# A recurrence inside a projection stream: a full-width state product, and output products issued once per quarter

## The chip, the core and the metric

The kernel runs on one core of one Trainium2 chip. The metric is the device time of one execution in microseconds, from launch to end; lower is better. [...] DMA queues move data between DRAM and SBUF.

## The reference

One layer of a decoder trunk is applied to a prompt of 1024 tokens and to 8 single-token samples, with a model width of 2048. After a norm, one projection (2048 to 8320 columns) feeds two groups of heads. Group A is an RWKV-7 time mixing with 16 heads of 64; group B is a retention with 4 heads of 256. The outputs are mixed, projected back, gated and normed. What the change touches is the recurrence of group A:

```python
def step(S, inp):
    r_t, w_t, k_t, v_t, a_t, b_t = inp
    sa = jnp.einsum('bhvk,bhk->bhv', S, a_t)
    S = S * w_t[:, :, None, :] + sa[..., None] * b_t[:, :, None, :] + v_t[..., None] * k_t[:, :, None, :]
    y = jnp.einsum('bhvk,bhk->bhv', S, r_t)
    return S, y
```

## The kernel before

All big projections are computed as three fp16 products (high times high, high times low, low times high) and run as one stream, the main stream: for each block of 128 output columns there are 3 token groups of 344, and for each of these 16 x 3 matmuls into a bank `pj` (`proj_gen`, `mm3`; the tiles are `u`, `mix` or `hh` for the activations and `whi`, `wlo` for the weights). Everything else is woven into this stream.

The weaving is done when the kernel is built. A `Driver` keeps an estimated clock for every engine. The main stream yields after every three matmuls. Then `poll` runs each background generator that is due: its next instructions are appended to the engines' queues at that place. A generator is due again 0.2 us after the estimated end of what it issued last, on any engine:

```python
b[0] = max(b[2].last + 0.2 if b[2].last else 0.0, self.t + w if isinstance(w, float) else 0.0, self.t)
```

The estimate of a product depends on the columns of its moving operand alone:

```python
n = rhs.free_size()
dv.op("PE", max((4 * n if lhsT.dtype == F32 else n) / 2400.0 + 0.0025, 0.025), [out], [lhsT, rhs])
```

On the chip each engine works through its queue in the written order and waits for semaphores.

Group A is handled in eight pairs of heads, p = 0 to 7. The tokens of a pair form 16 chunks of 64, and four chunks make a quarter. `front_gen` makes the quarters' inputs: `ar` (128 rows: two heads of 64; the first 64 of its 128 columns belong to the decayed removal keys, the last 64 to the receptances), `bk`/`bn` (the keys) and `x` (masked scores, whose triangular part is replaced by an inverse that VectorE solves, with a round trip through DRAM). `uv` holds per chunk the solved vectors u in rows 0 to 63 and the values v in rows 64 to 127.

`chain_gen` is the recurrence, in order over the 16 chunks of a pair. One chunk has three stages with a `yield` between them, so matmuls of the main stream stand between the stages:

1. The state's product (`ch<-Sbd,AR`, 128 rows and 64 columns of weights) is accumulated onto the product of scores and values that was issued one chunk earlier (`a2v`, `ch<-UV,X`). VectorE copies the sum to `R`.
2. The inverse is applied to `R` (`ch<-R,X`), VectorE copies the result into `uv`, and `a2v` of the next chunk is issued.
3. The update product (`ch<-UV,BN`), two VectorE instructions that make the new state `Sbd`, and the products for the output y: state by receptances (`y<-AR,Sbd`) and, for each head, `uv` by scores (`y<-X,UV`). Eight chunks share one bank `y`, which ScalarE and VectorE empty after the eighth.

All these products are fp32. An fp32 product appears in the trace as two matmuls, each with its own weight load. PSUM banks for the chain (`ch`) come from a pool of two, the bank `y` from a pool of one. The rings of `ar`, `x`, `bn` and `uv` come free when a quarter is marked done (`chq`), after its fourth chunk.

Of the kernel before, what the change touches and what calls it, by code (L numbers as in the profile page):

```python
# [10 lines left out]
F32 = mybir.dt.float32  # L11
F32R = mybir.dt.float32r
I32 = mybir.dt.int32
AF = mybir.ActivationFunctionType
ALU = mybir.AluOpType
PSUM = bass.MemoryType.PSUM

P = 128
# [244 lines left out]
def hybrid(ctx, tc, A):  # L263
    nc = tc.nc
    dv = Driver()
    V, S_, G = Eng(dv, "DVE", nc.vector), Eng(dv, "ACT", nc.scalar), Eng(dv, "POOL", nc.gpsimd)
# [3 lines left out]
    def pool(name, bufs=1, space=None, c=None, side=None):  # L270
        kw = {} if space is None else {"space": space}
        if side:
            kw["side"] = side
        return PoolProxy(dv, (c or ctx).enter_context(tc.tile_pool(name=name, bufs=bufs, **kw)), bufs)
# [11 lines left out]
    def mm(out, lhsT, rhs, **kw):  # L286
        n = rhs.free_size()
        dv.op("PE", max((4 * n if lhsT.dtype == F32 else n) / 2400.0 + 0.0025, 0.025), [out], [lhsT, rhs])
        PE.matmul(out, lhsT, rhs, **kw)  # L289
# [515 lines left out]
    two = pool("a2", 2, c=cr, side="right")  # L805
# [41 lines left out]
    def scr(i, dt=F32):  # L847
        return scp.tile([P, HB], dt, name=f"S{i}" if dt == F32 else f"R{i}", tag=f"S{i}")

# [103 lines left out]
    def front_gen(p):  # L953
# [116 lines left out]
        while p and ("chq", 4 * p - 1) not in done:  # L1070
            yield 0.3
        yield from chain_gen(p)

    def bkn_gen(p):
# [59 lines left out]
    def chain_gen(p):  # L1134
        DC = H["dc", p]

        def a2v(c):
            g, ci = 4 * p + c // 4, c % 4
            while ("uv", g) not in done or ("bkn", g) not in done:
                yield 0.3  # L1140
            ps = chp.tile([P, 512], F32, name="ch")
            x, uv = H["x", g], H["uv", g]
            for h in range(2):
                mm(ps[0:64, h * 64:h * 64 + 64], x[64:128, h, ci, 0:64], uv[64:128, ci, h * 64:h * 64 + 64],
                   start=h == 0, stop=c == 0 and h == 1, skip_group_check=True)
            return ps
        nxt = yield from a2v(0)
        for c in range(16):
            hf, g, ci = c // 8, 4 * p + c // 4, c % 4
            x, uv, bn, ar = (H[n, g] for n in ("x", "uv", "bn", "ar"))  # L1150
            if c % 8 == 0:
                ts = slice(hf * HB, hf * HB + HB)
                yps = yp.tile([P, 512], F32, name="y")
            S0, S1 = Sbd[c % 2], Sbd[1 - c % 2]
            ps = nxt
            if c:
                mm(ps[0:64, 0:P], ar[:, ci, 0:64], S0, start=False, stop=True, skip_group_check=True)
            R = two.tile([64, P], F32, name="R")
            V.tensor_copy(out=R, in_=ps[0:64, 0:P])
            yield  # L1160
            for h in range(2):
                mm(ps[0:64, P + h * 64:P + h * 64 + 64], x[0:64, h, ci, 0:64], R[:, h * 64:h * 64 + 64],
                   start=True, stop=True)
            V.tensor_copy(out=uv[0:64, ci, :], in_=ps[0:64, P:2 * P])
            if c < 15:
                nxt = yield from a2v(c + 1)
            yield
            mm(ps[:, 2 * P:3 * P], bn[:, ci, :], uv[:, ci, :], start=True, stop=True)
            for h in range(2):
                hs = slice(h * 64, h * 64 + 64)  # L1170
                src = ps[hs, 2 * P + h * 64:2 * P + h * 64 + 64]
                if c:
                    V.scalar_tensor_tensor(out=S1[hs, hs], in0=S0[hs, hs], scalar=DC[hs, c:c + 1],
                                           in1=src, op0=ALU.mult, op1=ALU.add)
                else:
                    V.tensor_copy(out=S1[hs, hs], in_=src)
            ysl = yps[:, (c % 8) * 64:(c % 8) * 64 + 64]
            if c:
                mm(ysl, S0, ar[:, ci, 64:128], start=True, stop=False, skip_group_check=True)
            for h in range(2):  # L1180
                hs = slice(h * 64, h * 64 + 64)
                mm(ysl[hs], uv[:, ci, hs], x[:, h, ci, 64:128], start=c == 0, stop=True, skip_group_check=True)
            if ci == 3:
                done.add(("chq", g))
            if c % 8 == 7:
                while not (p == 0 and hf == 0) and ("norm", p if hf else p - 1, 1 - hf) not in done:
                    yield 0.3
                Yh = og.tile([P, HB], F32R, name="Yh")
                Yl = og.tile([P, HB], F32R, name="Yl")
                S_.activation(Yh, yps, AF.Copy)  # L1190
                V.tensor_tensor(out=Yl, in0=yps, in1=Yh, op=ALU.subtract)
                done.add(("chain", p, hf))
                dv.spawn(norm(p, hf, Yh, Yl, ts))
            yield
        for h in range(2):
            hs = slice(h * 64, h * 64 + 64)
            SP.dma_start(out=A["o_wkvp"][2 * p + h], in_=Sbd[0][hs, hs])

    def norm(p, hf, Yh, Yl, ts):
        while ("gA", p) not in done:  # L1200
            yield 0.3
        yield when(Yl, 0.1)
        yield "g"
        yc = gtile()
        mm_exact(yc, cent_r, Yh, Yl)
        y2 = og.tile([P, HB], F32, name="y2")
        Y = og.tile([P, HB], F32, name="Y")
        S_.activation(y2, yc, AF.Square)
        S_.activation(Y, yc, AF.Copy)
        Yh = og.tile([P, HB], F32R, name="Yh")  # L1210
        Yl = og.tile([P, HB], F32R, name="Yl")
        halves(y2, Yh, Yl)
        yield when(Yl, 1.4)
        yield "g"
        yv = gtile()
        mm_exact(yv, bones_r, Yh, Yl)
        gt = og.tile([P, HB], F32, name="gt", tag="Yh")
        SP.dma_start(out=gt, in_=d_gate[p][:, ts])
        S_.activation(y2, yv, AF.Ln, scale=1.0 / 64, bias=eps_a[:, 0:1])
        S_.activation(y2, y2, AF.Exp, scale=-0.5)  # L1220
        yield
        V.tensor_tensor(out=Y, in0=Y, in1=y2, op=ALU.mult)
        bo = og.tile([P, HB], F32, name="bo", tag="Yl")
        SP.dma_start(out=bo, in_=d_bon[p][:, ts])
        V.tensor_scalar(out=Y, in0=Y, scalar1=vcol("gn_a_g", p), scalar2=vcol("gn_a_b", p), op0=ALU.mult, op1=ALU.add)
        yield
        G.tensor_tensor(out=Y, in0=Y, in1=bo, op=ALU.add)
        G.tensor_tensor(out=Y, in0=Y, in1=gt, op=ALU.mult)
        SP.dma_start(out=d_mxa[p][:, ts], in_=Y)
        done.add(("norm", p, hf))  # L1230
# [930 lines left out]
```

## Time and profile before

| | |
|---|---|
| median of 3 runs | 2767.7 us (2762.01 to 2771.42) |
| profiled execution | 2758.49 us, span of its instructions 2756.7 us |
| mean granted TensorE clock | 0.981 of full speed |
| TensorE / VectorE / ScalarE / GpSimd busy | 96% / 60% / 40% / 18% of the span |
| the pairs' chains | first `ch<-UV,X` at 269.2 us, last at 1425.6 us |

Busy time is the union of an engine's instructions. Matmuls are pipelined: the next one starts before the printed end of the one before, so what a matmul costs in a full queue is the distance between starts. In the timeline, neighbours of one form are merged into one row with a count; its first number is the start of the first of them, its second the time to the end of the last.

### The profile page before, as it was taken

Reading aid. Unit: us, or ns where it says so; the run is one execution under the profiler, and the core shown is the slowest. Engines: PE = TensorE matmul, PEld = TensorE weight load, DVE = VectorE, ACT = ScalarE, POOL = GpSimd, SP = SyncE. Lnnn points to the kernel's source line nnn. Section 1 sums busy time; section 2 is a strip of 40 time slices with the busy share of each in tenths; the row PEclk is TensorE's granted clock in tenths of the full one; section 3 lists DMA queues with packets and bytes.
Section 4 is the critical chain, followed back from the end, with each engine's and each line's share of the span. In section 5 each row is a group of like instructions: output and inputs, shape, how many; then the busy total and the mean of one; then the engine's idle time right before and its main releaser. Section 6 shows DMA issues by size and latency. Waiting matters only on the chain. (4 is left out here: it accounts for less than half of the span.)

```text
span 2756.7 us, 46895 instructions
## 1 busy us (share of the span) xinstructions
PE 2634.9 (96%) x19480; PEld 1774.0 (64%) x19480; DVE 1662.9 (60%) x3522; ACT 1114.5 (40%) x1563; POOL 508.0 (18%) x558
## 2 busy tenths in 40 slices
PE   7999999999999999999899999999999999999997
PEld 4566666666666666666567667676766666666664
DVE  7568687868577686867544867636365434353334
ACT  7543444343353434434224235443343323344333
POOL 3322122112121222212110321101000000033333
PEclk9999999999999999999899999999999999999998
DMA  7222121312222131222323435616163222333214
GB/s 267 75 79 61 53 82 40 95 35 78 60 85 55 53 99 30 82 60 82 93 78 119 168 134 191 218 66 209 47 223 129 94 106 100 131 123 108 101 69 139
DMA packets 146741, 283.63 MB, mean 103 GB/s; under 512 B 62568, under 2 KB 100520, under 8 KB 131424
## 3 DMA queue, kind: packets, MB, share of 16 engines
q1 hardware_dynamic: 132160, 178.91, 19.7%
q10 hardware_dynamic: 14368, 101.73, 10.9%
q8 instruction: 152, 2.49, 0.4%
q14 instruction: 61, 0.50, 0.1%
HBM read 212.78 MB, written 67.55 MB: 102 GB/s over the span
## 5 line engine op out<-in xcount | busy, mean ns | idle before, releaser
L289 PE MATMUL pj<-u,whi 128*128 128x344 f16 x6176 | 1388.5, 313 | 29.0 <-DVE sgt L244 16.1
L289 PEld LDWEIGHTS <-whi 128*128 128x128 f16 x9408 | 883.1, 99 | 494.7 <-issue 73.0
L289 PE MATMUL pj<-u,wlo 128*128 128x344 f16 x3088 | 959.1, 312 | 0.0
L289 PEld LDWEIGHTS <-wlo 128*128 128x128 f16 x4704 | 463.7, 99 | 233.3 <-DVE wlo L244 1.5
L244 DVE SCALAR_TENSOR_TENSOR wlo<-raw,so,whi 128x512 f16<-128x512 f32 (+1 forms) x398 | 294.1, 772 | 80.8 <-ACT whi L244 80.4
L289 PE MATMUL pj<-hh,whi 128*128 128x344 f16 (+3 forms) x1536 | 335.2, 309 | 0.2 <-ACT whi L244 0.2
L289 PE MATMUL pj<-mix,whi 128*128 128x344 f16 x1504 | 330.8, 310 | 1.5 <-DVE hr L244 1.5
L244 ACT ACTIVATE whi<-raw,so 128x1024 f16<-128x1024 f32 (+2 forms) x200 | 217.6, 1121 | 125.4 <-DVE so L244 118.1
L289 PE MATMUL pj<-hh,wlo 128*128 128x344 f16 (+3 forms) x768 | 237.3, 309 | 0.4 <-DVE wlo L244 0.4
L289 PE MATMUL pj<-mix,wlo 128*128 128x344 f16 x752 | 230.1, 310 | 0.4 <-DVE wlo L244 0.4
L244 ACT ACTIVATE wjunk<-raw 128x2048 f16<-128x2048 f32 x94 | 177.2, 1885 | 100.2 <-DVE raw L244 63.4
L244 ACT ACT_TABLE_LOAD x136 | 174.5, 1283 | 16.5 <-DVE R L244 11.4
L244 POOL TENSOR_TENSOR H<-H,sgt 128x344 f32<-128x344 f32 (+3 forms) x45 | 59.5, 1322 | 552.8 <-DMA xr<-d_ple 363.2
L244 DVE TENSOR_TENSOR tm<-LT,Z 128x8 f32<-128x8 f32 (+15 forms) x128 | 138.7, 1084 | 2.0
L244 ACT ACTIVATE z<-pj,winv 128x344 f32<-128x344 f32 x74 | 40.3, 547 | 240.0 <-PE pj L289 191.1
L244 DVE TENSOR_TENSOR sgt<-sgt,xr 128x344 f32<-128x344 f32 (+3 forms) x48 | 25.8, 538 | 159.5 <-ACT sgt L244 157.6
L244 POOL TENSOR_TENSOR d<-z 128x344 f32<-128x344 f32 (+1 forms) x75 | 63.1, 842 | 253.7 <-ACT z L244 174.4
L244 ACT ACTIVATE sgt<-pj,winv 128x344 f32<-128x344 f32 (+4 forms) x93 | 50.7, 545 | 144.7 <-PE pj L289 128.7
L244 DVE SCALAR_TENSOR_TENSOR Sbd<-Sbd,DC,ch 64x64 f32<-64x64 f32 x240 | 66.4, 277 | 53.5 <-PE ch L289 50.3
L244 DVE SCALAR_TENSOR_TENSOR hr<-pj,winv,xr 128x344 f32<-128x344 f32 x47 | 26.9, 575 | 111.2 <-PE pj L289 107.8
L244 POOL TENSOR_TENSOR rl<-y,rh 128x344 fp32r<-128x344 f32 x24 | 27.2, 1133 | 345.8 <-DVE rh L244 177.0
L244 DVE TENSOR_REDUCE Z<-tm 128x4 f32<-128x8 f32 (+15 forms) x128 | 86.5, 676 | 4.4
(319 smaller groups left out, 3325.4 us busy)
## 6 DMA issues: line engine op xcount, KB each, us to landing
raw<-in_w_in ACTq DMA_DIRECT2D x63, 1024.0 KB, 5.1
raw<-in_w_out ACTq DMA_DIRECT2D x16, 1024.0 KB, 4.8
raw<-in_w_gate ACTq DMA_DIRECT2D x16, 1024.0 KB, 4.8
x<-in_xT SPq DMA_DIRECT2D x16, 516.0 KB, 10.3
tb<-in_rq SPq DMA_DIRECT2D x24, 344.0 KB, 5.0
tb<-in_rk SPq DMA_DIRECT2D x24, 344.0 KB, 3.7
xr<-in_xT SPq DMA_DIRECT2D x16, 516.0 KB, 4.2
d_h<-hr SPq DMA_DIRECT2D x16, 516.0 KB, 2.9
```

The costliest lines, as they stand in the source:

```text
L244: return f(*a, **k)
L289: PE.matmul(out, lhsT, rhs, **kw)
```

## The change

Three edits in `chain_gen`:

- `a2v` closes its accumulation. Except for chunk 0, ScalarE copies its result from PSUM to a new SBUF tile `AV` (64x128).
- The state's product takes all 128 columns of `ar` as weights and writes 128 rows into its own columns of the bank (the last 64 rows aren't read). VectorE makes `R` by adding `AV` to the first 64 rows, in place of a copy.
- The two `y<-X,UV` products of each chunk are no longer issued in that chunk. After the fourth chunk of a quarter, all eight of the quarter are issued. The bank `y` is opened by the first product of state by receptances (chunk 1 or 8) alone, and everything after it accumulates or, on columns not written since, overwrites.

```diff
--- before.py
+++ after.py
@@ -1142,8 +1142,12 @@
             x, uv = H["x", g], H["uv", g]
             for h in range(2):
                 mm(ps[0:64, h * 64:h * 64 + 64], x[64:128, h, ci, 0:64], uv[64:128, ci, h * 64:h * 64 + 64],
-                   start=h == 0, stop=c == 0 and h == 1, skip_group_check=True)
-            return ps
+                   start=True, stop=True, skip_group_check=True)
+            av = None
+            if c:
+                av = two.tile([64, P], F32, name="AV")
+                S_.activation(av, ps[0:64, 0:P], AF.Copy)
+            return ps, av
         nxt = yield from a2v(0)
         for c in range(16):
             hf, g, ci = c // 8, 4 * p + c // 4, c % 4
@@ -1152,11 +1156,13 @@
                 ts = slice(hf * HB, hf * HB + HB)
                 yps = yp.tile([P, 512], F32, name="y")
             S0, S1 = Sbd[c % 2], Sbd[1 - c % 2]
-            ps = nxt
+            ps, av = nxt
+            R = two.tile([64, P], F32, name="R")
             if c:
-                mm(ps[0:64, 0:P], ar[:, ci, 0:64], S0, start=False, stop=True, skip_group_check=True)
-            R = two.tile([64, P], F32, name="R")
-            V.tensor_copy(out=R, in_=ps[0:64, 0:P])
+                mm(ps[:, 3 * P:4 * P], ar[:, ci, :], S0, start=True, stop=True, skip_group_check=True)
+                V.tensor_tensor(out=R, in0=ps[0:64, 3 * P:4 * P], in1=av, op=ALU.add)
+            else:
+                V.tensor_copy(out=R, in_=ps[0:64, 0:P])
             yield
             for h in range(2):
                 mm(ps[0:64, P + h * 64:P + h * 64 + 64], x[0:64, h, ci, 0:64], R[:, h * 64:h * 64 + 64],
@@ -1176,10 +1182,13 @@
                     V.tensor_copy(out=S1[hs, hs], in_=src)
             ysl = yps[:, (c % 8) * 64:(c % 8) * 64 + 64]
             if c:
-                mm(ysl, S0, ar[:, ci, 64:128], start=True, stop=False, skip_group_check=True)
-            for h in range(2):
-                hs = slice(h * 64, h * 64 + 64)
-                mm(ysl[hs], uv[:, ci, hs], x[:, h, ci, 64:128], start=c == 0, stop=True, skip_group_check=True)
+                mm(ysl, S0, ar[:, ci, 64:128], start=c in (1, 8), stop=False, skip_group_check=True)
+            if ci == 3:
+                for j in range(4):
+                    yq = yps[:, (c % 8 - 3 + j) * 64:(c % 8 - 2 + j) * 64]
+                    for h in range(2):
+                        hs = slice(h * 64, h * 64 + 64)
+                        mm(yq[hs], uv[:, j, hs], x[:, h, j, 64:128], start=False, stop=True, skip_group_check=True)
             if ci == 3:
                 done.add(("chq", g))
             if c % 8 == 7:
```

## Rows read from the trace of the kernel before

**Rows 1.** The page, part 1: busy us, share of the span, instructions.

```profile
PE 2634.9 (96%) x19480; PEld 1774.0 (64%) x19480; DVE 1662.9 (60%) x3522; ACT 1114.5 (40%) x1563; POOL 508.0 (18%) x558
```

**Rows 2.** Stretches: length, busy PE, PEld, DVE, ACT, POOL, clock, DMA share, GB/s.

```profile
250.00:1440.00 1190.00, 1145.23 (x9331) 752.21 (x9330) 834.08 (x1812) 468.50 (x647) 226.15 (x288) 0.98 0.23 69
...
650.00:722.00 72.00, 68.21 (x551) 46.01 (x551) 51.65 (x95) 27.55 (x43) 11.26 (x16) 0.95 0.27 82
```

**Rows 3.** Instructions on tile ch: duration ns min/median/max, first and last start.

```profile
L289 PEld LDWEIGHTS ch<-UV,BN x256: 186/189/226, 271.7 to 1430.2; 128*128 128x128 f32 x128
...
L289 PEld LDWEIGHTS ch<-Sbd,AR x240: 132/136/227, 273.5 to 1427.7; 128*64 128x64 f32 x120
L289 PE MATMUL ch<-Sbd,AR x240: 272/323/477, 273.5 to 1427.8; 128*64 128x128 f32 x120
...
L244 DVE COPY R<-ch x128: 216/282/284, 269.8 to 1428.1; 64x128 f32<-64x128 f32 x128
```

**Rows 4.** Instructions on tile y, columns as in rows 3.

```profile
L289 PE MATMUL y<-X,UV x512: 222/270/370, 272.2 to 1430.8; 128*64 128x64 f32 x171
```

**Rows 5.** Timeline of TensorE, third stage of a chunk: start us, us, instruction.

```profile
619.99 0.47 PE L289 MATMUL ch<-UV,BN 128*128 128x128 f32 x2
620.30 0.33 PE L289 MATMUL y<-AR,Sbd 128*128 128x64 f32 x2
620.56 0.34 PE L289 MATMUL y<-X,UV 128*64 128x64 f32 x4
620.83 0.47 PE L289 MATMUL pj<-u,whi 128*128 128x344 f16 x2
```

**Rows 6.** Timeline of TensorE, first and second stage of the next chunk.

```profile
621.13 0.31 PE L289 MATMUL pj<-u,wlo 128*128 128x344 f16 x1
621.37 0.43 PE L289 MATMUL ch<-Sbd,AR 128*64 128x128 f32 x2
621.74 0.47 PE L289 MATMUL pj<-u,whi 128*128 128x344 f16 x2
...
623.15 0.27 PE L289 MATMUL ch<-R,X 64*64 64x64 f32 x1
...
623.39 0.22 PE L289 MATMUL ch<-UV,X 64*64 64x64 f32 x1
```

**Rows 7.** Timeline of TensorE around a pair of 128-column fp32 passes.

```profile
202.63 0.31 PE L289 MATMUL pj<-u,wlo 128*128 128x344 f16 x1
202.78 0.38 PE L294 MATMUL g<-con,F 128*128 128x128 f32 x2
202.99 0.46 PE L289 MATMUL pj<-u,whi 128*128 128x344 f16 x2
```

**Rows 8.** Timeline of TensorE around two passes with 64 columns of data.

```profile
1462.34 0.33 PE L289 MATMUL g<-dm,exact 128*128 128x64 f32 x2
1462.51 0.46 PE L289 MATMUL pj<-u,whi 128*128 128x344 f16 x2
```

**Rows 9.** Waits of TensorE in 250 to 1440: us in total, times, longest.

```profile
PE pj L289 <- DVE sgt L244: 16.1, 5, 4.2
PE g L289 <- DMA XN<-d_X: 10.1, 4, 5.5
...
PEld ch L289 <- DVE UV L244: 18.9, 63, 2.1
```

**Rows 10.** Groups of ScalarE by form: busy us, mean ns, idle before.

```profile
L244 ACT ACTIVATE wjunk<-raw 128x2048 f16<-128x2048 f32 x92 | 175.1, 1904 | 94.3 <-DVE raw L244 63.4 <-DMA raw<-in_w_in 30.6
L244 ACT ACT_TABLE_LOAD x136 | 174.5, 1283 | 16.5 <-DVE R L244 11.4 <-PE g L289 1.4 <-PEq L2149 0.7
...
L244 ACT ACTIVATE UV<-g 64x256 f32<-64x256 f32 x32 | 12.1, 379 | 71.0 <-DVE UV L244 70.8
```

## The prediction

> **What bounds the kernel now.** I read the page first: TensorE is busy for 96% of the span, ScalarE for 40% [rows 1]. Busy time of TensorE says little by itself, because matmuls overlap, so the second view is the stretches: the recurrence runs between about 250 and 1440 us, and there TensorE is busy for 1145 of 1190 us, VectorE for 834 [rows 2]. The third view is the waits of TensorE in that stretch. The longest groups are 16 us for an evicted projection bank and 10 us for a load from DRAM [rows 9]; nothing there waits for long on the recurrence's own products. So in the stretch of the change the kernel ends when TensorE has worked through its queue, in the written order, and a microsecond of TensorE taken out is a microsecond of span, as long as no other engine is then late. The view that prices the change is therefore the timeline of TensorE, read by **starts**: the distance from one matmul's start to the next is what the queue pays, not the printed duration.
>
> A projection matmul of 344 columns starts 0.15 us after the one before it. Against this, one step of the recurrence looks as follows. After the update product `ch<-UV,BN` come two matmuls `y<-AR,Sbd`, four `y<-X,UV`, and the next projection matmul starts 0.53 us after the first `y<-AR,Sbd` [rows 5]. Then the state's product `ch<-Sbd,AR`, two matmuls with 64 columns of weights: the projection matmul before it starts at 621.13 and the one after it at 621.74, 0.61 us in place of 0.15 [rows 6]. The same pair of passes with 128 columns of weights, a pair of transposes between projection matmuls, takes 202.63 to 202.99, 0.36 us [rows 7]. So the narrow product is the dearer one. It is late at both edges: it starts 0.24 us after the projection matmul before it, where 0.15 is usual, and the next projection matmul starts 0.37 us after it. The group `ch<-R,X`, `ch<-UV,X`, with 64 rows and 64 columns, also starts late, and four-matmul `y<-X,UV` starts 0.26 us after `y<-AR,Sbd` although the latter is only 64 columns wide [rows 5, 6]. What these have in common is a change between full-width and half-width use of the array, and the loss stands at each such change.
>
> **The change, part by part.**
>
> The state's product. There are 240 matmuls in 120 products (chunk 0 of each of the eight pairs has none) [rows 3]. Each goes from 0.61 to 0.36 us by the rows above, 0.25 us less: 120 x 0.25 = 30.0 us. One thing could make it less. The product waits for VectorE's state, and `ch<-UV,BN`, full-width and just released by VectorE in the row shown, takes 0.31 us to the next group where 128-column pairs take 0.21 [rows 5, 7]. If each product pays that 0.1 us, 12 us are lost and 18 remain. I take 30, since the moment of release depends on the order and the row shows a near miss.
>
> The Trainium skill (TensorE: Matmul & The Clock Gate, section LDWEIGHTS) speaks against this part: it says that a weight load takes a time in proportion to its columns, at 1.2 columns per ns, whatever the rows. By that rule the load goes from 53 to 107 ns, and two passes in 120 products would cost 13 us more, if nothing hid them. The trace agrees that the load is longer (medians of 136 and 189 ns, both in [rows 3]), but the pair of 128-column passes in [rows 7] holds its two loads and still costs 0.36 us from projection matmul to projection matmul. By the rule with the load exposed this part would give 17 us, by the row 30.
>
> The products for y. All 512 matmuls `y<-X,UV` stay [rows 4]; what falls away is their position in 96 of 128 chunks (three of four). There `y<-AR,Sbd` will be followed by a projection matmul, or by another full-width group. The nearest row is two matmuls of the same form, 128 rows and columns of weights and 64 columns of data, of which the first starts at 1462.34 and the projection matmul after them at 1462.51: 0.17 us, where it is 0.53 now [rows 5, 8]. That saves 0.36 us, and 96 x 0.36 = 34.6 us. (Chunk 0 has no `y<-AR,Sbd`, I take the same saving there.) In the fourth chunk 16 matmuls stand where four stood. Their entry and exit are already paid, so the question is what three more sets of four cost. From above: 0.27 us a set, the whole of the set in the row, edges included, or 32 x 3 x 0.27 = 26 us. From below: eight half-width matmuls of the step before start within 623.15 to 623.39, two at a time, so four in 0.12 us [rows 6], and the two heads of y go to separate halves of the array's columns in the same way: 32 x 3 x 0.12 = 11.5 us. I take the latter, because the two first `y<-X,UV` overlap too: four of them are over in 0.34 us [rows 5].
>
> The eviction AV: 120 new ScalarE copies of 64x128 from PSUM. The nearest row is a copy of 64x256, 0.38 us [rows 10]; with half the elements it lies between half of that and all of it, and I take the middle, 0.28, so 34 us on an engine that is 40% busy [rows 1]. It is hidden by the interval from the `uv` products to the state's product. The update product alone starts 1.38 us before it (619.99 to 621.37) [rows 5, 6] and AV's source is written before that. If that cover is gone, R waits for AV, and behind R on VectorE everything waits; the price is in the rivals.
>
> The add in place of the copy for R: a copy of 64x128 is 0.28 us [rows 3]. The add reads the same PSUM columns; between 0.28 and twice that, I take 0.28. It lies between the state's product and `ch<-R,X`, 1.78 us apart in the row (621.37 to 623.15) and filled with projection matmuls [rows 6].
>
> The order. The kernel's driver prices a product by its data columns alone, so the wider weights don't change its plan. AV does: the next step is due 0.2 us after the later of UV's copy and AV, which by the driver's own costs is about 0.2 us later than now, often one more set of three projection matmuls. That lengthens the chain a little, and moves the update product away from UV's copy, on whose release the weight loads now wait 63 times, 18.9 us in all [rows 9]; a part of these could go, up to some 5 us. I leave it out of the sum and keep it for the range. The y bank, opened once, moves no work; its eviction after chunks 7 and 15 starts later by the batch, and nobody near waits for it.
>
> Sum: 30.0 + 34.6 - 11.5 = 53 us. The gain in TensorE's queue is 7 us per pair. What is late next are the waits that don't shrink with TensorE: VectorE solves the triangular systems between chains (51.65 of 72 us busy in 650 to 722) while TensorE waits for evictions and for the solve's round trip through DRAM [rows 2, 9]. I let 2 us come back in all. Gain 51 us. The profiled execution took 2758.5 us (span 2756.7), so its counterpart would be about 2707. It was 9 us faster than the median of the runs, 2767.7; taken off that, the forecast is 2717 us.
>
> **The rivals.**
>
> *The saved time comes back as waits.* Each pair's chain depends, through the front and the solve, on the chain before it, and these steps run on VectorE, ScalarE and the DMA queues, which the change doesn't shorten. The kernel has run behind its driver's plan in every product (0.46 us more than the projection matmuls alone, planned 0.22), and this hid late inputs. For it: in the solve's stretch TensorE already stands still, 16.1 us in five waits and 10.1 in four [rows 9]. Against it: both together are 26 us over eight pairs, and few waits stand inside the chains. If half of the 53 us comes back, the time is 2741.
>
> *The change doesn't do what it says.* The late starts might come from the semaphore that each of these groups waits for, not from the width. Then the state's product gains nothing, and the batch as little as it saves, about 2767. Against it: `y<-X,UV` waits for nothing new, and its first start is late all the same [rows 5]; and the projection matmul after the state's product, which waits for nothing either, is late by 0.22 us [rows 6].
>
> *Slower: AV is late.* AV stands in ScalarE's strict order. A squared-sum pass over the weights of 1.9 us and a table load of 1.28 us [rows 10] can stand ahead of it, 3.2 us against the 1.38 us of cover, so R can be 1.8 us late, VectorE with it, and TensorE waits at `ch<-R,X`. If this befalls 60 of 120 products, it costs 108 us, net 55 slower: 2823. It decides from a mean lateness of 0.44 us per product (53/120). Against it: the driver knows ScalarE's queue and puts the next step off until AV is done in its plan, so the projection matmuls fill most of such a delay.
>
> **How the numbers follow.** A change of under 0.3%, about 8 us, can't be told from none here. Chances: forecast 0.62, with its own range 2705 to 2730 (gain 38 with the batch at its upper end, 59 to 63 with the waits on UV gone and nothing given back); returned waits 0.22, 2730 to 2760; no effect 0.08; slower 0.08. The range leaves out the last two and the far end of the second, some 0.19: 2700 to 2752. Faster by over 0.3%: 0.84; within: 0.08; slower: 0.08.
>
> **What would show it.** In the profile after, `ch<-Sbd,AR` must be a 128x128 form with the projection matmuls around it 0.36 us apart; a chunk without `y<-X,UV` must return to projection matmuls 0.17 us after the first `y<-AR,Sbd`; 16 `y<-X,UV` must start within about 0.5 us. TensorE's two groups of waits in [rows 9] must stay near their 26 us, and R must seldom wait for AV. The prediction is wrong if TensorE's waits in this stretch grow by more than 15 us, if the 16 take over 0.8 us, or if the edges stay at 0.24 and 0.37 us.

## Result, and the profile after

The changed kernel takes 2731.2 us (median of 4 runs, 2728.67 to 2735.15) against 2766.0 us for the kernel before (4 runs on the same chip), a ratio of 0.988 with a 95% interval of 0.9865 to 0.9895. That is 35 us faster, where 51 were forecast: inside the range as a whole (2700 to 2752), but 1 us outside the forecast's own 2705 to 2730, at the edge of the 2730 to 2760 that the returned waits were given. The profiled executions stand at 2728.67 and 2758.49 us, 29.8 us apart.

The page's first part, of the kernel after: busy us, share of the span, instructions. It answers to [rows 1]. (PE is TensorE, which does the matrix products, and PEld its weight loads; DVE is VectorE and ACT ScalarE, for element-wise work and for emptying the banks; POOL is GpSimd.)

```profile
PE 2593.1 (95%) x19480; PEld 1779.4 (65%) x19480; DVE 1660.2 (61%) x3522; ACT 1152.0 (42%) x1691; POOL 526.7 (19%) x558
```

TensorE lost 42 us of busy time with the same number of matmuls, and the span became 30 us shorter: so TensorE stands still more than before.

Now the instructions on tile `ch` and on tile `y` of the kernel after, as in [rows 3] and [rows 4]: durations in ns (min/median/max).

```profile
L289 PEld LDWEIGHTS ch<-Sbd,AR x240: 186/190/338, 272.0 to 1424.2; 128*128 128x128 f32 x120
L289 PE MATMUL ch<-Sbd,AR x240: 272/275/551, 272.0 to 1424.3; 128*128 128x128 f32 x120
...
L244 ACT ACTIVATE AV<-ch x120: 253/270/273, 269.4 to 1422.2; 64x128 f32<-64x128 f32 x120
L244 DVE TENSOR_TENSOR R<-ch,AV x120: 270/282/284, 272.5 to 1424.6; 64x128 f32<-64x128 f32 x120
```

```profile
L289 PE MATMUL y<-X,UV x512: 221/222/370, 282.9 to 1427.5; 128*64 128x64 f32 x171
```

The product is in the 128x128 form, the weight load is longer (190 ns where 136 stood), the add for R costs what the copy cost, and AV takes 0.27 us.

The timeline of TensorE in the kernel after, read by starts as in [rows 5, 6]: the fourth chunk of a quarter with its batch of 16, and, after the dots, a chunk without `y<-X,UV` and its state product.

```profile
618.54 0.31 PE L289 MATMUL pj<-u,wlo 128*128 128x344 f16 x1
618.69 0.38 PE L289 MATMUL ch<-UV,BN 128*128 128x128 f32 x2
618.91 0.33 PE L289 MATMUL y<-AR,Sbd 128*128 128x64 f32 x2
619.17 0.69 PE L289 MATMUL y<-X,UV 128*64 128x64 f32 x16
619.79 0.47 PE L289 MATMUL pj<-u,whi 128*128 128x344 f16 x2
...
1264.32 0.33 PE L289 MATMUL y<-AR,Sbd 128*128 128x64 f32 x2
1264.49 0.46 PE L289 MATMUL pj<-u,whi 128*128 128x344 f16 x2
...
1265.22 0.31 PE L289 MATMUL pj<-u,wlo 128*128 128x344 f16 x1
1265.37 0.38 PE L289 MATMUL ch<-Sbd,AR 128*128 128x128 f32 x2
1265.59 0.46 PE L289 MATMUL pj<-u,whi 128*128 128x344 f16 x2
```

The reader is to see four distances. The state's product costs 1265.22 to 1265.59, 0.37 us from projection matmul to projection matmul (0.61 before). After `y<-AR,Sbd` alone the stream goes on after 0.17 us (0.53 before). The 16 matmuls of the batch take 619.17 to 619.79, 0.62 us, where four took 0.27: three more sets cost 0.35 us. And `ch<-UV,BN` is followed after 0.22 us, where 0.31 stood.

So the unit prices came as worked out. The waits didn't. Those of TensorE in 250 to 1440 us, kernel after, as in [rows 9]:

```profile
PE g L289 <- DVE R L244: 17.1, 6, 2.9
PE ch L289 <- DVE Sbd L244: 13.6, 18, 1.4
PE g L289 <- POOL z L244: 9.0, 6, 1.7
PE g L294 <- ACT UV L244: 8.2, 6, 1.4
...
PE g L289 <- DMA XN<-d_X: 1.8, 1, 1.8
```

The two groups of [rows 9] are all but gone (26.2 to 1.8 us), and other ones, 48 us together, stand in their place. Six each are for a VectorE cast and for GpSimd's work behind it: both make an operand of the next pair's front, and both are late where VectorE ends a pair's solve. Six are for ScalarE's copy of the values into `uv`, and 18 for the recurrence's state. The first three come once per pair, 5.7 us together. Stretches of the kernel after, columns as in [rows 2], show where five of the last lie, 3.7 us:

```profile
250.00:1440.00 1190.00, 1132.60 (x9520) 776.64 (x9519) 837.67 (x1827) 513.38 (x785) 244.90 (x291) 0.97 0.23 69
1266.30:1298.00 31.70, 22.95 (x147) 16.89 (x145) 17.53 (x50) 6.57 (x15) 7.00 (x6) 0.62 0.17 53
```

The second stretch is a halt. In the kernel before, TensorE is busy for nearly all of these same microseconds:

```profile
1266.30:1298.00 31.70, 31.63 (x255) 21.17 (x255) 23.95 (x61) 6.71 (x12) 5.35 (x4) 0.98 0.32 106
```

In the kernel after, for 31.7 us, the second half of the seventh pair's chain runs with no projection matmul between its steps; the main stream has come to its first block of group B, which by the written order waits for a step of the eighth pair's preparation, and that comes after this chain. TensorE is busy for 22.95 us of it and, after it had stood still three times, is granted a mean clock of 0.62: half speed (1.2 GHz) from 1269.8 us for 23.9 us. The chain's steps there, TensorE's timeline of the kernel after, with the idle time ahead and what ended it in brackets:

```profile
1267.48 0.49 PE L289 MATMUL ch<-UV,BN 128*128 128x128 f32 x2 [0.36 <-DVE UV L244]
1267.80 0.33 PE L289 MATMUL y<-AR,Sbd 128*128 128x64 f32 x2
1268.74 0.46 PE L289 MATMUL ch<-Sbd,AR 128*128 128x128 f32 x2 [0.61 <-DVE Sbd L244]
1269.58 0.27 PE L289 MATMUL ch<-R,X 64*64 64x64 f32 x1 [0.38 <-DVE R L244]
```

Bare, one chunk waits three times for VectorE, 1.35 us in all. Elsewhere projection matmuls hide nearly all of these.

**The accounting** used below. All kernels are compared over the same work: from the first matmul of the main stream's 9th block to that of its 51st. "Idle" is that length less TensorE's busy time. "Clock" is half of the time for which TensorE was busy at 1.2 GHz (what it lost against 2.4). "Work" is the rest: the queue's own time. "Between" is the number of projection matmuls that stand between the inverse's product (`ch<-R,X`) and the update product (`ch<-UV,BN`), over all 128 chunks. "Chain" is the mean time from a pair's first to its 16th update product, over the first seven pairs. Where the work of one kind of product is given below, it is summed over the same stretch: each distance from a start to the next, less idle time and clock, and what a group starts later behind a projection matmul than the usual 0.146 us is counted as the group's. The stretches of before and after, columns as in [rows 2]:

```profile
255.69:1608.81 1353.12, 1303.18 (x10397) 865.57 (x10395) 938.77 (x2033) 527.67 (x735) 258.87 (x308) 0.98 0.24 76
```

```profile
253.95:1575.91 1321.96, 1261.37 (x10397) 870.53 (x10395) 935.10 (x2032) 565.64 (x864) 273.75 (x308) 0.98 0.25 78
```

| kernel | length | idle | clock | work | between | chain |
|---|---|---|---|---|---|---|
| before | 1353.1 | 49.9 | 25.7 | 1277.5 | 657 | 78.4 |
| after | 1322.0 | 60.6 | 25.7 | 1235.7 | 1152 | 80.4 |
| state edit alone | 1311.3 | 43.2 | 17.9 | 1250.2 | 1014 | 75.4 |
| y edit alone | 1319.0 | 41.2 | 22.7 | 1255.1 | 699 | 72.9 |
| after, AV not due | 1339.1 | 73.3 | 32.0 | 1233.8 | 693 | 73.9 |
| after without AV | 1299.1 | 43.3 | 13.5 | 1242.3 | 684 | 72.9 |
| same, idle AV | 1347.6 | 75.7 | 28.7 | 1243.3 | 981 | 80.0 |
| same, idle AV not due | 1309.4 | 51.6 | 11.0 | 1246.9 | 687 | 73.2 |
| same, copy of R | 1324.0 | 59.6 | 21.9 | 1242.5 | 840 | 73.7 |
| state edit without AV | 1330.3 | 48.1 | 21.6 | 1260.6 | 594 | 74.6 |

Before to after: 41.8 us of work gone, 10.7 us of idle time come back; the net is 31.1 us, and the two executions are 29.8 us apart. The chain, with less to do in each step, has become 2 us longer, and the column "between" says why: 495 more projection matmuls stand in that one gap, about 3.9 per chunk. AV's due time in the driver is the suspect; the tests below switch it.

**Theories.** *Due time:* AV puts the step after it off in the driver's plan, so the chain and what hangs on it (the next pair's solve, the halt ahead of group B) move against the main stream, and waits come back. *Sizes:* the products are worth only some 60% of what was worked out. *On the chip:* R, or a product, really waits for AV. A fourth came later, *load*: the 120 copies on ScalarE delay other evictions.

### The profile page after: what moved, and what is told of

It is laid out like the page before. It is cut to its first block, busy times and chain, and to the rows that moved or that the text cites. A ratio compares the mean times of both kernels' runs of the same rounds, so it can differ in the third digit from the quotient of the medians.

```text
span 2726.8 us, 47191 instructions
## 1 busy us (share of the span) xinstructions
PE 2593.1 (95%) x19480; PEld 1779.4 (65%) x19480; DVE 1660.2 (61%) x3522; ACT 1152.0 (42%) x1691; POOL 526.7 (19%) x558
## 4 chain that ended last, share of the span: by engine, by line
PE 72%; DVE 18%; issue 4%; POOL 2%; ACT 2%; DMA 2%; SPq 0%; POOLq 0%; ACTq 0%; DVEq 0%
PE pj L289 57%; PE ch L289 7%; PE g L289 5%; DVE tm L244 5%; DVE Z L244 2%; PE y L289 2%; DVE wlo L244 2%; PE g L294 1%; DVE F L244 1%; DVE S L244 1%; POOL u L244 1%; DVE Y L244 1%; POOL H L244 1%; DVE Sbd L244 1%; DVE UV L244 0%
## 5 line engine op out<-in xcount | busy, mean ns | idle before, releaser
L289 PEld LDWEIGHTS <-whi 128*128 128x128 f16 x9408 | 897.7, 99 | 457.2 <-issue 41.7
L244 ACT ACTIVATE AV<-ch 64x128 f32<-64x128 f32 x120 | 32.2, 268 | 241.8 <-PE ch L289 241.6
L244 DVE TENSOR_TENSOR sgt<-sgt,xr 128x344 f32<-128x344 f32 (+3 forms) x48 | 26.2, 545 | 161.3 <-ACT sgt L244 159.4
```

What stands on the lines that cost most here:

```text
L244: return f(*a, **k)
```

## The experiments

They ran in three groups, each with the kernel before on the same chip: each edit alone, AV not due and the first gate version beside 2764.6 us (7 runs); the second gate version, the front's step and the two without AV beside 2765.2 us (7 runs); the rest beside 2762.9 us (13 runs). The ratios are against these.

**Each edit alone.** In the first, the y products go back into their chunks; in the second, the state's product goes back to the narrow form and AV goes.

```diff
 # e1_state_only, from after
-                mm(ysl, S0, ar[:, ci, 64:128], start=c in (1, 8), stop=False, skip_group_check=True)
-            if ci == 3:
-                for j in range(4):
...
+                mm(ysl, S0, ar[:, ci, 64:128], start=True, stop=False, skip_group_check=True)
+            for h in range(2):
+                hs = slice(h * 64, h * 64 + 64)
+                mm(ysl[hs], uv[:, ci, hs], x[:, h, ci, 64:128], start=c == 0, stop=True, skip_group_check=True)
 # e2_y_only, from after
-            ps, av = nxt
+            ps = nxt
...
+                mm(ps[0:64, 0:P], ar[:, ci, 0:64], S0, start=False, stop=True, skip_group_check=True)
+            R = two.tile([64, P], F32, name="R")
+            V.tensor_copy(out=R, in_=ps[0:64, 0:P])
```

> The state's product in full width with AV, as in the change; the products for y as before, in every chunk. Theory 1 (the plan): TensorE's queue is cheaper by what the rows say, but AV puts each step of the recurrence off, so the pairs' chains fall behind the main stream, and the saved time comes back in one piece where the main stream must wait for the last pair before group B's first block. Then TensorE's work falls by about 28 us, the chain of a pair stays near 80 us from first to last update product, and the time is 2745 to 2758. Theory 2 (the sizes): the edits save on TensorE only some 60% of what was worked out, evenly over the pairs, and nothing comes back. Then it is 2748 to 2752 with no stretch without projection matmuls near the end of pair 6's chain. The trace tells them apart, the time hardly.

> The products of uv by scores once per quarter, the bank opened once; the state's product as before (64 columns, accumulated, no AV). Theory 1: TensorE's work falls by about 23 us, the chain isn't put off, so no stretch without projection matmuls appears and nearly all arrives: 2740 to 2747. Theory 2 (60% of the worked-out size): 2751 to 2755.

Measured: state edit alone 2723.6 us, ratio 0.9853 (0.9838 to 0.9867); y edit alone 2726.2 us, 0.9862 (0.9848 to 0.9877). Each by itself beats the two together. Both times lie below every range that was expected for them. In work they gave 27.3 and 22.4 us (forecast 30.0 and 34.6 - 11.5 = 23.1), so the theory of sizes falls. Each also made idle and clock together smaller by 12 to 15 us (61.1 and 63.9 us against 75.6); only with both edits did they grow (86.3). The longest waits of the two kernels, in 250 to 1440 us, first the state edit, then the y edit:

```profile
PE g L289 <- DMA XN<-d_X: 23.9, 6, 6.3
```

```profile
PE g L289 <- DMA XN<-d_X: 21.9, 7, 5.7
```

So in these two the solve's round trip through DRAM is what comes late, once per pair, as the prediction's first rival had it, and in the kernel after it hardly is (1.8 us): which step of the solve or of the front is late changes with the order.

**AV taken out of the due time.** The driver's note of when the step's work ends is put back after AV is issued.

```diff
 # e4_av_not_due, from after
+                was = dv.cur.last
                 S_.activation(av, ps[0:64, 0:P], AF.Copy)
+                dv.cur.last = was
```

> The change, but the driver doesn't count AV when it sets the due time of the recurrence's next step; the same instructions, only their order differs. Theory 1: the chain of a pair shortens from 80.6 us to 73 to 78, it stays closer to the main stream, and the halt of 31 us before group B shrinks to under 20: 2710 to 2724. Theory 2: the order makes no difference, 2728 to 2735. Theory 3 (R waits for AV on the chip): more waits for ACT AV, 2735 or more.

Measured: 2746.8 us, ratio 0.9934 (0.9919 to 0.9949), 16 us slower than the whole change and in the range expected from the theory of a wait on the chip. "Between" fell to 693 and the chain to 73.9 us, and still idle time rose by 12.7 us. Waits of this kernel in 250 to 1440 us:

```profile
PE g L289 <- DMA XN<-d_X: 34.8, 5, 7.2
PE ch L289 <- ACT AV L244: 7.7, 6, 1.3
```

Two things are seen: without the put-off, TensorE does wait for AV on the chip, though for 7.7 us only; and the solve's round trip is late again, and by more than in any other kernel. The due-time theory in its simple form, a shorter chain and the time is back, falls here. The test isn't clean, though: in the driver's plan R still waits for AV, and what hangs on R moves with it.

**The halt.** The main stream has five blocks per pair; the fifth, from the second pair on, computes a gate of group B. Two versions take these blocks one pair later, all or only the last, so that the stream has other work where it stood still.

```diff
-    GB_AFTER = {p: (p - 1,) for p in range(1, 8)}
+    GB_AFTER = {**{p: (p - 2,) for p in range(2, 7)}, 7: (5, 6)}    # e5_gate_later
+    GB_AFTER = {**{p: (p - 1,) for p in range(1, 6)}, 7: (5, 6)}    # e8_gate_last
```

> The change, with the gate blocks of group B that are mixed into pairs 1 to 7 put one pair later (none in pair 1, two in pair 7), so that the main stream delivers every pair's inputs a block earlier and has one more block to run while the last pair's chain ends. Theory 1: the halt before group B's first block shrinks from 31 us to 15 or less and the time is 2708 to 2720. Theory 2: no halt matters, 2728 to 2735.

> The change, with one gate block of group B moved from pair 6 to pair 7, so that one more block stands between pair 7's inputs and group B's first block. Theory 1: the change's cheaper queue is partly lost in the halt of 31.7 us at 1266 (idle time and half clock there are worth some 20 us), because the main stream runs ahead of the last chains; the block covers most of the halt: 2711 to 2719. Rival: the halt moves elsewhere at the same price, as it did to pair 0 when all gate blocks were put later: 2728 to 2735.

Measured: 2735.2 us (0.9896, 0.9879 to 0.9912) and 2732.7 us (0.9888, 0.987 to 0.9907), no better than the whole change at 2731.2. The halt didn't go, it moved. Stretches, first of the former, then of the latter:

```profile
318.70:348.80 30.10, 21.51 (x164) 16.69 (x163) 15.81 (x47) 6.81 (x15) 5.83 (x6) 0.69 0.19 58
1266.30:1298.00 31.70, 31.69 (x278) 22.39 (x278) 21.40 (x62) 10.47 (x24) 6.05 (x4) 1.00 0.30 98
```

```profile
1105.80:1135.50 29.70, 21.54 (x165) 16.54 (x164) 15.83 (x47) 6.85 (x15) 5.82 (x6) 0.66 0.19 58
```

Where the halt was, TensorE is now busy for 31.69 of 31.70 us; in another pair's chain, just before the pair that has lost its fifth block, stands a halt of 30 us. A stream that is ahead of the chains stops somewhere, so the place of the halt isn't where the time goes.

**A step of the front put off.** The waits for R, where a pair's solve ends, might be filled by starting the product of the front that waits there later.

```diff
 # e9_front_due, from after
+            yield when(rl, 1.4)
             yield "g"
             pn = gtile()
```

> The change, and in the front the norm's product of a pair is due only when its second operand is done by the plan. In the change's trace TensorE waits there 2.9 and 1.4 us in each of six pairs and is granted half clock for some 6.8 us after it. Theory 1 (these waits are tight places of the plan that cost what they show): 4 to 7 us per pair come free, 2692 to 2708. Rival (TensorE only waits where something else is late anyway; the front is put off, and with it the solve and the chain): 2722 to 2740.

Measured: 2744.9 us, ratio 0.993 (0.991 to 0.9951), 14 us slower, and slower than either theory had it. The wait for R grew from 17.1 to 27.4 us. Longer distances in the plan cost here too.

**Without AV.** The wide product accumulates onto the product of scores and values, in the same columns, and VectorE copies R as before the change. To have all 128 rows of these columns open, two banks of PSUM (the memory that TensorE's products are written to) are held per pair and opened once each by a product; the last 64 rows still aren't read.

```diff
 # e10_wide_no_av, from after
+            if c < 2:
+                held.append(chp.tile([P, 512], F32, name="ch"))
+                mm(held[c][:, 0:P], ident, ident, start=True, stop=True, skip_group_check=True)
+            ps = held[c % 2]
...
-                av = two.tile([64, P], F32, name="AV")
-                S_.activation(av, ps[0:64, 0:P], AF.Copy)
...
-                mm(ps[:, 3 * P:4 * P], ar[:, ci, :], S0, start=True, stop=True, skip_group_check=True)
-                V.tensor_tensor(out=R, in0=ps[0:64, 3 * P:4 * P], in1=av, op=ALU.add)
+                mm(ps[:, 0:P], ar[:, ci, :], S0, start=False, stop=True, skip_group_check=True)
+            V.tensor_copy(out=R, in_=ps[0:64, 0:P])
 # e11_wide_no_av_gate_last: the same with the second GB_AFTER from above
```

> The change without AV: the full-width state product accumulates onto the scores' product in place, as before the change, in two banks that are held for a pair's whole chain and whose other 64 rows are first written by one product each (16 small products more in all); VectorE copies the sum to R as before. Theory (AV puts the steps off, so the chains run late): TensorE's work is that of the change, the chain of a pair takes 72 to 76 us in place of 80.6, there is no halt before group B: 2708 to 2720. Rival (AV has no part in it): 2726 to 2736.

> The last two of these ideas together: no AV, and one gate block of group B moved from pair 6 to pair 7. If the kernel without AV has no halt before group B, nothing is left for the moved block to cover and the time is that of the kernel without AV within 6 us; if it has one, some 10 to 20 us less.

Measured: 2710.6 us, ratio 0.981 (0.979 to 0.9831), the fastest of all; with the later gate 2718.4 us, 0.9834 (0.9814 to 0.9853), 7.8 us more, where the same time within 6 was expected: the gate is again worth nothing. Its waits in 250 to 1440 us are those of [rows 9] again, and little besides, and the stretch runs at 0.99 of full clock:

```profile
PE pj L289 <- DVE sgt L244: 15.0, 5, 5.1
PE g L289 <- DMA XN<-d_X: 9.7, 4, 3.2
PE ch L289 <- DVE R L244: 2.9, 7, 1.3
```

```profile
250.00:1440.00 1190.00, 1152.07 (x9742) 795.36 (x9741) 846.94 (x1887) 491.05 (x682) 244.10 (x292) 0.99 0.24 74
```

It saves 6.6 us less of work than the whole change (1242.3 against 1235.7; the 16 products that open its banks take 5.9) and loses 29.5 us less to idle time and clock (56.8 against 86.3). So AV, with the add that it needs and without the held banks, costs 23 us net in that stretch. The version without it gains 55 us in all, about what the queue was forecast to give, but not from there alone: 35.2 us of it are work, 18.8 are idle time and clock. What of AV costs, the next three take apart.

**AV put back, idle.** Onto the version without AV: a copy of the same product, which nobody reads (the state's product, which writes the same columns, comes after it); the same without its due time; and a copy of R, in SBUF and ready before, in its place.

```diff
 # e12_idle_av, from e10_wide_no_av, after the product of scores and values
+            if c:
+                av = two.tile([64, P], F32, name="AV")
+                S_.activation(av, ps[0:64, 0:P], AF.Copy)
 # e13_idle_av_not_due: the same, between was = dv.cur.last and dv.cur.last = was
 # e14_av_of_r, from e10_wide_no_av, after the call of a2v for the next chunk
+                av = two.tile([64, P], F32, name="AV")
+                S_.activation(av, R, AF.Copy)
```

> The version without AV (2711 us), with AV put back as a copy that nobody reads: same source, same place in ScalarE's queue, same driver cost, and the state's product, which writes the columns that it reads, still comes after it. Due-time theory (AV moves the recurrence's steps to a later place among the projection matmuls, and that shifts the solve's waits): 2727 to 2735 us, as with the whole change, and the chain's step again as even as there. R theory (the sum on VectorE, or its wait for AV, is what costs): R is a plain copy here, so 2707 to 2715 us. ScalarE-load theory (120 copies of 0.27 us delay other evictions): 2727 to 2735 us.

> As the idle copy, but the driver's due time of the next step is put back to what it was before the copy. Due-time theory: 2707 to 2717 us, plus what the state's product then waits for AV on the chip (8 us when this was done to the whole change). ScalarE-load theory: 2727 to 2735 us, no different from the idle copy that counts.

> The idle copy reads R, which is in SBUF and ready long before, in place of the product: its load on ScalarE is the same, but no step comes due later for it and no product waits for it. Due-time theory: 2707 to 2715 us. ScalarE-load theory: 2727 to 2735 us.

Measured: idle AV 2756.6 us, 0.9981 (0.9971 to 0.999); not due 2720.9 us, 0.986 (0.9838 to 0.9882); copy of R 2725.3 us, 0.9869 (0.9852 to 0.9886). The idle copy costs 46 us, far more than either theory had, and all but 10 of it are gone when the driver doesn't count it (the version without AV ran on another chip; by the ratios it is 47 and 14). The two kernels differ in the driver's due time alone. Waits of the two in 250 to 1440 us, first the idle AV that counts, then the one that doesn't:

```profile
PE g L289 <- DVE R L244: 27.2, 6, 4.6
PE ch L289 <- DVE Sbd L244: 12.5, 10, 1.5
PE ch L289 <- DVE R L244: 7.6, 18, 0.7
...
PE g L289 <- DMA XN<-d_X: 2.0, 1, 2.0
```

```profile
PE pj L289 <- DVE sgt L244: 14.5, 5, 5.3
PE g L289 <- DMA XN<-d_X: 8.8, 4, 3.1
PE ch L289 <- ACT AV L244: 6.2, 7, 1.5
```

The first has the pattern of the kernel after, its even chains (80.2 us in six pairs), its six waits for R, its halt (at 1295.0 us, 28.9 us long); the second has the pattern without AV, plus 6.2 us of waits for AV on the chip. Work differs by 3.6 us, idle and clock by 41.8. So in this form due time is the main cause, shown by switching it alone; the wait on the chip is real and small. The theory that R's add or its wait is what costs falls, since R is a plain copy in all three. Load isn't cleared: the copy of R was meant to leave the due times alone, but "between" rose to 840, and it shows 24.2 us of waits on the solve's round trip; its 15 us, between the ranges of the two theories, can't be divided between load and order.

**The state edit without AV.** The y products go back into each chunk of the version without AV.

```diff
 # e15_state_no_av: e10_wide_no_av with the y products of the kernel before
```

> The version without AV, with the y products back in each chunk. If what the y edit gives doesn't depend on AV, it costs its work again, 20 to 23 us: 2731 to 2735 us. Rival: AV was worth something to the state edit, since with AV the update product no longer waits for its weight load (0.085 us per step, some 10 us in all), and this version is slower still: 2738 to 2745 us. Rival: the y edit brings its own waits, and this version is as fast as the state edit with AV: 2720 to 2727 us.

Measured: 2737.0 us, ratio 0.9919 (0.9893 to 0.9946), between the first two expectations. Against the state edit with AV (2723.6, on another chip) it is slower by 13 us and has 10.4 us more of work. AV's put-off is also worth something: waits of the weight loads, first of the state edit with AV, then without:

```profile
PEld ch L289 <- DVE UV L244: 2.1, 5, 0.6
```

```profile
PEld ch L289 <- DVE UV L244: 16.3, 73, 1.1
```

The update product, released late, no longer meets a load that waits: the group `ch<-UV,BN`, `y<-AR,Sbd`, `y<-X,UV` takes 0.762 us out of the stream (median of 85 undisturbed ones with AV) where it takes 0.848 without (82), 0.086 us less. (That is the distance from the start of the projection matmul before the group to the second one after it, less two strides of 0.146.) For 73 such waits that makes 6.3 us, and the update products' work says the same, 30.8 us with AV and 37.4 without. The other large difference is the 16 opening products, 5.9 us, which only the version without AV needs; smaller ones go both ways.

## Why the prediction came out as it did

**The bound.** Right: TensorE's queue bounds the stretch, and cutting it shortens the span.

**The state's product, 30.0 us.** 21.5 came: its work fell from 54.1 to 32.7 us. The unit price held (0.24 us less per product by the rows above, 0.25 forecast), the count didn't. Of 120 products 58 stand alone between projection matmuls after, and 51 of these cost 0.37 us. 20 stand directly behind the 16 score products (`g<-AR,BK`, 64 rows of weights). Such a place on TensorE's timeline, before and then after:

```profile
288.80 1.16 PE L289 MATMUL g<-AR,BK 64*128 64x128 f32 x16
289.89 0.43 PE L289 MATMUL ch<-Sbd,AR 128*64 128x128 f32 x2
290.26 0.47 PE L289 MATMUL pj<-u,whi 128*128 128x344 f16 x2
```

```profile
287.88 1.16 PE L289 MATMUL g<-AR,BK 64*128 64x128 f32 x16
288.98 0.49 PE L289 MATMUL ch<-Sbd,AR 128*128 128x128 f32 x2
289.30 0.46 PE L289 MATMUL pj<-u,whi 128*128 128x344 f16 x2
```

Both forms start 1.09 us after the first score product, and the projection matmul follows after 0.365 us with the narrow one and after 0.325 with the wide one, against 0.22 where the wide one stands alone: 0.04 us saved, not 0.25. Shared edges were left out of the step.

The 27.3 us of work that the state edit gave alone are near the 30.0 by luck: 21.7 are the state's product, and 6.2 stand at the update product, whose weight loads hardly wait for UV any more. Without AV the edit gave 16.9 (1277.5 - 1260.6), since those 6.2 are missing and the opening products cost 5.9. The near miss that I named (0.31 us in place of 0.21 at `ch<-UV,BN`) mostly didn't come: seven of the 58 cost 0.55 us or more. At `ch<-UV,BN` itself it went: behind a projection matmul 51 of 85 showed it before, two of 87 after.

The Trainium skill (TensorE: Matmul & The Clock Gate, section LDWEIGHTS) has a load's time in proportion to its columns. Here its median rose from 136 to 190 ns, 1.4 times, where the columns doubled. Exposed it was not, since 0.37 us from projection matmul to projection matmul are, within 0.01, what the pair of transposes of [rows 7] takes.

**The products for y, 34.6 - 11.5 = 23.1 us.** Right: their work fell by 22.3 us, with 0.17 us after `y<-AR,Sbd`, and 0.35 us for three more sets (0.36 forecast by the lower end; the upper was 0.81).

**The queue, 53 us.** 41.8 came: 21.5 from the state's product, 22.3 from y, and 5.6 from the update product, whose loads wait for UV 13 times in place of 63; I had left that out of the sum, at "up to some 5 us". All other groups together cost 7.6 us more. Part of it can be counted: 27 groups of score products stand behind a projection matmul, where they start 0.24 us after it, and eight did before (1.8 us); of the groups `ch<-R,X`, `ch<-UV,X`, 131 do and 118 did (1.6 us). So a narrow group that stood behind another one now pays its own edge. The rest is spread over small groups and wasn't followed up.

**"I let 2 us come back in all."** This is the step that failed: 10.7 us came back as idle time, and against what each edit alone did with its waits (61.1 and 63.9 us of idle and clock) it is over 20. I had written that AV delays the next step "by about 0.2 us", "often one more set of three projection matmuls", and "lengthens the chain a little", and priced that at nothing. It was on the mark as a mechanism, 3.9 matmuls per chunk. What it did was not a little: six chains took an even 80.5 to 80.8 us, the waits moved from evictions and the DRAM round trip to the operands of the next pair's front, where VectorE ends a solve, and a halt of 31.7 us appeared. That the put-off makes this pattern is shown by the idle copy, counted and not counted. That it alone costs the whole change its 10.7 us is not shown: there, with the put-off taken away, idle time rose by another 12.7 us.

**The rivals.** Returned waits, at 2741 for half of the 53 us, was the nearest other case, and a fifth of 53 is what came back; with the 11 us that the queue didn't give, the time, 2731.2, lies in this rival's range by 1 us. The sign that I had set, waits grown by more than 15 us, was nearly met: TensorE's idle time in 250 to 1440 us grew from 44.8 to 57.4. "Doesn't do what it says" is out by the unit prices. AV late on the chip: none of TensorE's longer waits after is for AV, which in all 120 products had ended at least 1.7 us before the state's product did; where the put-off was taken away there were 6 to 8 us of them, far from the 53 from which it decides.

**Still open:** why the whole change without AV's due time is slower (2746.8) when the idle copy without it is faster (2720.9). Both have short chains; in the former the solve's DRAM round trip is late by 35 us, in the latter by 9. I know where these waits stand, but not which step of the front or of the solve decides which pattern a version falls into.

## What to carry to other kernels

In a kernel whose order is planned, an instruction that looks free because its engine is idle has a second price: the planner counts its end, and everything queued behind that end moves. Switch the planner's count alone, as with the idle copy, before blaming the chip. And price a narrow product by its neighbours: what is saved by widening it is the two changes of width, and where a neighbour is narrow too, one of them was never paid, and the wide product now pays its own.

## What the runs showed of the hardware

A change between full-width and half-width fp32 products cost about 0.09 us on the way in (0.24 us in place of 0.15) and, for the state's product, 0.15 us on the way out (0.37 in place of 0.22, by the rows above); a product with half the weights was dearer by 0.24 us than the full one. Directly behind products with 64 rows of weights the difference was 0.04 us. A weight load that waited for VectorE's copy cost the queue about 0.09 us where no matmul shows a wait: in the state edit without AV, the matmuls after `ch<-UV,BN` were late by that in 63 of 71 groups with such a load and in 8 of 34 without. Sixteen narrow matmuls in a row cost 0.12 us per four. The granted clock fell to 1.2 GHz during the waits where a pair's solve ends (at 553.0 us, in a wait of 2.87 us that ended at 553.3), for 6.8 us in five pairs and 3.4 in one, and stayed there for 23.9 us in the halt, where TensorE was busy for 22.95 of 31.7 us.
